# Holding an early store back until the last load has landed, in a log-sum-exp kernel that streams its input

One core of one Trainium2 chip. The metric is the device time of one execution in microseconds (us), median of several.

## The reference

The input is 32 x 512 rows of 1024 floats (67.1 MB), the output one float per row (65.5 KB).

```python
def reference(x):                       # x: (32, 512, 1024) float32
    max_x = np.max(x, axis=-1, keepdims=True)
    return (max_x.squeeze(-1) + np.log(np.sum(np.exp(x - max_x), axis=-1))).astype(np.float32)
```

## The kernel before

Each partition gets 128 rows ("columns" of the result): 112 from the first part of the input and 16 from the rest, so that the output is two contiguous blocks. SyncE issues 16 loads into a ring in SBUF, large ones first, of one row per partition at last. ScalarE takes the exponential without subtracting a maximum, VectorE or ScalarE sums, ScalarE takes Ln. A check at the end branches to a safe path if a sum is out of range (never taken here). What the change touches, cut:

```python
    for i, (size, ops) in enumerate(loads):
        ...
        dma = nc.sync.dma_start(out=ring[:, here : here + size], in_=source(done, size)).ins
        ...                                    # exponentials (line 143 with sum, 148 without), sums (160, 165)
        if c == LATE:                          # 119 columns are summed
            ln = nc.scalar.activation(out=res[:, 0:W], in_=sumexp[:, 0:W], func=AF.Ln)     # line 184, W = 112
            ...
    nc.at_finalize(wait_for_store_in_barrier)  # GpSimd, not SyncE, waits for last_store, in the closing barrier

    nc.scalar.activation(out=res[:, W:NC], in_=sumexp[:, W:NC], func=AF.Ln)               # line 232
    nc.sync.dma_start(out=out_rows, in_=res[:, 0:W])                                       # line 233, the first store
    last_store = nc.sync.dma_start(out=out_rest, in_=res[:, W:NC]).ins                     # line 234, the final store
```

SyncE executes its instructions in program order: 16 loads, first store, final store. In the loop's last turn `dma` is the last load.

## Time and profile before

| | before |
|---|---|
| time, median of the first 3 runs | 163.46 us (163.31 to 163.52) |
| span of the profiled execution | 161.5 us |
| queue q1 (all loads and stores), share of 16 engines | 97.1% |
| last load landed | 157.90 us |
| ScalarE busy without a gap from | 153.50 us |
| first store issued / landed | 150.80 / 158.1 us |
| final store issued / landed | 159.35 / 160.77 us |

Landing times in this table are the trace's own; the prediction below, which shows the lines and follows the end of the span back, adds figures rounded to 0.1 us and so has 157.87 and 160.75.

### The profile page before, as it was taken

What the parts mean: (1) busy time and instruction counts of PE and PEld (TensorE: products, weight loads), DVE (VectorE), ACT (ScalarE), POOL (GpSimd) and SP (SyncE); (2) the same over time, 40 slices, a digit from 0 to 9 for tenths busy, and PEclk for the clock granted to TensorE, in tenths of its full rate; (3) what the DMA queues carried; (4) which work ended last, traced back from release to release, by engine and by line L of the source; (5) the groups of instructions that cost most, each with busy time, mean ns of one, the idle gap of its engine ahead of it and who ended that gap; (6) DMA issues with size and microseconds to landing.
All of it is one profiled execution on the core that took longest, in us unless ns stands there. A gap on an engine that the chain in (4) does not pass through costs nothing.

```text
span 161.5 us, 257 instructions
## 1 busy us (share of the span) xinstructions
PE 1.9 (1%) x24; PEld 1.0 (1%) x24; DVE 114.9 (71%) x61; ACT 117.0 (72%) x59; POOL 0.2 (0%) x4
## 2 busy tenths in 40 slices
PE   0000000000000000000000000000000000000021
PEld 0000000000000000000000000000000000000011
DVE  0000000899929999399999999999499956996683
ACT  3000059990799609994299949974999999999994
POOL 0000000000000000000000000000000000000000
DMA  8997997997997997998899999997999999999990
GB/s 276 503 519 308 471 519 308 471 519 308 471 519 325 455 519 341 438 519 357 382 438 438 438 422 406 495 495 318 438 438 464 388 440 416 430 424 420 414 382 8
DMA packets 2594, 67.19 MB, mean 416 GB/s; under 512 B 544, under 2 KB 544, under 8 KB 928
## 3 DMA queue, kind: packets, MB, share of 16 engines
q1 hardware_dynamic: 2592, 67.18, 97.1%
q14 instruction: 2, 0.02, 0.0%
HBM read 67.11 MB, written 0.07 MB: 416 GB/s over the span
## 4 chain that ended last, share of the span: by engine, by line
DMA 59%; ACT 19%; DVE 16%; another core or an unknown queue 3%; issue 1%; SPq 0%; PE 0%
DMA ring<-in_x_dram 59%; ACT ring L148 19%; DVE sumexp L160 15%; DVE ring L165 1%; SPq L131 0%; DVE bad L238 0%; PE count L119 0%; DVE bad L239 0%; DVE fine L247 0%; PE count L246 0%; DVE clamped L115 0%; PE count L245 0%
## 5 line engine op out<-in xcount | busy, mean ns | idle before, releaser
L160 DVE TENSOR_REDUCE sumexp<-ring 128x8 f32<-128x8192 f32 (+6 forms) x17 | 102.9, 6107 | 39.6 <-ACT ring L148 39.6
L148 ACT ACTIVATE ring<-ring 128x8192 f32<-128x8192 f32 (+14 forms) x24 | 98.9, 4174 | 41.5 <-DMA ring<-in_x_dram 41.5
L143 ACT ACTIVATE ring<-ring 128x1024 f32<-128x1024 f32 x15 | 15.6, 1040 | 0.0
L165 DVE SCALAR_TENSOR_TENSOR ring<-ring 128x512 f32<-128x512 f32 x17 | 10.9, 687 | 3.5 <-ACT ring L148 3.5
L143 ACT ACTIVATION_READ_ACCUMULATOR ring<-ring 128x1 f32 x15 | 2.8, 186 | 0.0
L108 PE MATMUL count<-far,bad 128*1 128x1 f32 x2 | 0.2, 164 | 153.2 <-DVE clamped L104 153.2
L80 ACT ACT_TABLE_LOAD x1 | 1.3, 1283 | 0.8 <-PEq L309 0.8
L114 PE MATMUL count<-sumexp,ones 128*1 128x1 f32 x16 | 1.4, 164 | 3.9 <-DVE ring L165 3.9
L165 DVE DVE_READ_ACCUMULATOR ring<-ring 128x1 f32 x17 | 1.4, 82 | 0.0
L143 ACT ACTIVATE last_exp<-ring 128x1024 f32<-128x1024 f32 x1 | 1.0, 1005 | 0.0
L108 PEld LDWEIGHTS count<-far,bad 128*1 128x1 f32 x2 | 0.1, 80 | 153.2 <-DVE clamped L104 153.2
L114 PEld LDWEIGHTS count<-sumexp,ones 128*1 128x1 f32 x16 | 0.6, 81 | 4.6 <-DVE ring L165 4.6
L81 DVE MEMSET ones<- 128x1 f32 x1 | 0.1, 59 | 0.9 <-PEq L309 0.9
L247 DVE TENSOR_SCALAR fine<-count 1x1 int32<-1x1 f32 x1 | 0.1, 147 | 0.4 <-PE count L246 0.4
L104 DVE SCALAR_TENSOR_TENSOR clamped<-clamped,sumexp 128x119 f32<-128x119 f32 x1 | 0.3, 283 | 0.0
L238 DVE TENSOR_REDUCE bad<-ring 128x1 f32<-128x64 f32 x1 | 0.2, 220 | 0.1
L184 ACT ACTIVATE res<-sumexp 128x112 f32<-128x112 f32 x1 | 0.3, 278 | 0.0
L100 DVE TENSOR_SCALAR clamped<-sumexp 128x119 f32<-128x119 f32 x1 | 0.2, 221 | 0.0
L232 ACT ACTIVATE res<-sumexp 128x16 f32<-128x16 f32 x1 | 0.2, 215 | 0.0
L119 PE MATMUL count<-far,bad 128*1 128x1 f32 x2 | 0.2, 164 | 0.3 <-DVE clamped L115 0.3
L246 PE MATMUL count<-sumexp,ones 128*1 128x1 f32 x2 | 0.2, 164 | 0.0
L245 PE MATMUL count<-far,bad 128*1 128x1 f32 x2 | 0.2, 164 | 0.0
(13 smaller groups left out, 1.4 us busy)
## 6 DMA issues: line engine op xcount, KB each, us to landing
ring<-in_x_dram SPq DMA_DIRECT2D x1, 6912.0 KB, 31.7
ring<-in_x_dram SPq DMA_DIRECT2D x1, 6400.0 KB, 26.4
ring<-in_x_dram SPq DMA_DIRECT2D x1, 4608.0 KB, 25.1
ring<-in_x_dram SPq DMA_DIRECT2D x1, 3840.0 KB, 23.4
ring<-in_x_dram SPq DMA_DIRECT2D x1, 2816.0 KB, 25.8
ring<-in_x_dram SPq DMA_DIRECT2D x1, 2048.0 KB, 30.0
ring<-in_x_dram SPq DMA_DIRECT2D x1, 1792.0 KB, 22.5
ring<-in_x_dram SPq DMA_DIRECT2D x1, 1408.0 KB, 25.4
```

What stands on the lines that cost most here:

```text
L80: nc.scalar.preload_act_table_set("natural_log_exp_and_others")
L100: nc.vector.tensor_scalar(out=clamped[:, 0:LATE], in0=sumexp[:, 0:LATE], scalar1=LOW, scalar2=HIGH, op0=ALU.max, op1=ALU.min,)
L104: counted = nc.vector.scalar_tensor_tensor(out=clamped[:, 0:LATE], in0=clamped[:, 0:LATE], scalar=0.0, in1=sumexp[:, 0:LATE], op0=ALU.bypa ...
L108: nc.tensor.matmul(count, lhsT=bad[:, 0:1], rhs=far, start=True, stop=False)
L114: nc.tensor.matmul(count, lhsT=ones, rhs=sumexp[:, c : c + 1], start=False, stop=False)
L119: nc.tensor.matmul(count, lhsT=bad[:, 1:2], rhs=far, start=False, stop=False)
L143: exp = nc.scalar.activation(out=o, in_=v, func=AF.Exp, accum_out=sums)
L148: exp = nc.scalar.activation(out=v, in_=v, func=AF.Exp)
L160: added = [nc.vector.reduce_sum(out=sums, in_=rows, axis=AX.X)]
L165: nc.vector.scalar_tensor_tensor(out=lo, in0=lo, scalar=1.0, in1=rows[:, r, H:d], op0=ALU.mult, op1=ALU.add, accum_out=sums[:, r : r + 1],)
L184: ln = nc.scalar.activation(out=res[:, 0:W], in_=sumexp[:, 0:W], func=AF.Ln)
L232: nc.scalar.activation(out=res[:, W:NC], in_=sumexp[:, W:NC], func=AF.Ln)
```

## The change

Intent: "keeps its packets out of the last load's". The store of the first 112 columns, ready at 150.8 us while loads were still streaming, should not share the DMA engines with the last of them. It now waits for the last load, still ahead of the final store.

```diff
     nc.scalar.activation(out=res[:, W:NC], in_=sumexp[:, W:NC], func=AF.Ln)
-    nc.sync.dma_start(out=out_rows, in_=res[:, 0:W])
+    store = nc.sync.dma_start(out=out_rows, in_=res[:, 0:W]).ins
+    info = mybir.DependencyInfo(mybir.DependencyClass.Sync, mybir.DependencyReason.DATA)
+    tc.add_manual_dep(store, dma.name, info, reason="keeps its packets out of the last load's")
     last_store = nc.sync.dma_start(out=out_rest, in_=res[:, W:NC]).ins
```

## The prediction

> **What bounds the kernel now.** I read the page first, then the answers for the last 12 us, because the change touches only what SyncE does after it has issued all loads.
>
> The page says that the kernel is one stream of loads:
>
> ```profile
> GB/s 276 503 519 308 471 519 308 471 519 308 471 519 325 455 519 341 438 519 357 382 438 438 438 422 406 495 495 318 438 438 464 388 440 416 430 424 420 414 382 8
> q1 hardware_dynamic: 2592, 67.18, 97.1%
> HBM read 67.11 MB, written 0.07 MB: 416 GB/s over the span
> ```
>
> Loads and both stores are on one queue, q1, whose packets took 97.1% of 16 engines' span. Only the last of the 40 slices (4.04 us each) is empty: there the end is set by what follows the last data. The 0.07 MB written are both stores together, so all that the change can move is 0.056 MB out of 67.
>
> The DMA issues of the page give the two stores, and the source view of the load line over the last two issues gives the last two loads (their count and start, then time to landing, min/median/max):
>
> ```profile
> out_dram<-res SPq DMA_DIRECT2D x1, 56.0 KB, 7.3
> out_dram<-res SPq DMA_DIRECT2D x1, 8.0 KB, 1.4
> L131 SPq DMA_DIRECT2D ring<-in_x_dram x2: 327/380/432, 131.3 to 131.7; - x2
> DMA to landing us min/median/max: 25.4/25.8/26.2
> ```
>
> Asked for the issue at 131.30 alone, the DMA view gives 25.4, so the last but one landed at 131.30 + 25.4 = 156.70 and the last at 131.67 + 26.2 = 157.87. The gap, 1.17 us for 512 KB (0.524 MB), is 448 GB/s: the last load came at full rate, although the early store was outstanding.
>
> The timeline of ScalarE and of SyncE's queue from 153 us (start, duration, line):
>
> ```profile
> 153.50 3.50 ACT L148 ACTIVATE ring<-ring 128x2304 f32<-128x2304 f32 x2 [0.23 <-DMA ring<-in_x_dram]
> 156.91 1.04 ACT L143 ACTIVATE ring<-ring 128x1024 f32<-128x1024 f32 x1
> 157.85 0.19 ACT L143 ACTIVATION_READ_ACCUMULATOR ring<-ring 128x1 f32 x1
> 157.95 1.00 ACT L143 ACTIVATE last_exp<-ring 128x1024 f32<-128x1024 f32 x1
> 158.89 0.19 ACT L143 ACTIVATION_READ_ACCUMULATOR last_exp<-ring 128x1 f32 x1
> 159.11 0.21 ACT L232 ACTIVATE res<-sumexp 128x16 f32<-128x16 f32 x1
> ...
> 150.80 0.35 SPq L233 DMA_DIRECT2D out_dram<-res  x1
> 159.35 0.34 SPq L234 DMA_DIRECT2D out_dram<-res  x1
> ```
>
> From 153.50 on ScalarE runs back to back. Its last wait for a load is the 0.23 us before 153.50. The last row's exponential starts at 157.95, 1.04 us after the one before it, which is the plain spacing of this form on ScalarE (144.30, 145.33, 146.37 earlier in the timeline). Its data were there at 157.87. So the end runs: ScalarE busy from 153.50, Ln of the last 16 columns to 159.33, final store issued at 159.35, landed at 159.35 + 1.4 = 160.75, then the closing barrier to 161.5:
>
> ```profile
> L320 POOLq EVENT_SEMAPHORE  x4: 17/17/43, 160.8 to 161.4; - x4
> ```
>
> GpSimd's first barrier step, which holds the wait for the final store, begins at 160.8, just when that store has landed. The first store, issued at 150.80, landed at 150.80 + 7.3 = 158.1 and is on nobody's path.
>
> **What the Trainium skill says.** "DMA: Bandwidth & Descriptors", section Queues, rings and completion order: SP owns one queue row, and each DMA engine consumes that row's descriptors in ring order. So a store issued behind the last load should not start on an engine before that engine's share of the load. The trace agrees. The DMA view from 150.8 to 156.4:
>
> ```profile
> DMA packets 444, 2.29 MB, mean 410 GB/s; under 512 B 48, under 2 KB 48, under 8 KB 364
> ```
>
> Each DMA carries one packet of under 512 B per engine that counts its semaphore: on the whole page 544 = 18 DMAs x 16 + 128 rows of 448 B + 128 rows of 64 B. The 48 here are 3 loads x 16, so for 5.6 us after its issue not one packet of the store has moved.
>
> Same page, section Anatomy of one DMA: DMA engines do not wait on semaphores; the issuing sequencer does, before dispatch. So the new wait holds SyncE itself, and the final store behind it in SyncE's order. The trace of before agrees in kind: SyncE's own waits show it standing at the first store until ScalarE's Ln is done.
>
> ```profile
> SPq L233 <- ACT res L184: 12.6, 1, 12.6
> SPq L234 <- ACT res L232: 8.1, 1, 8.1
> ```
>
> Same page, same section: the fixed cost of a DMA is put at about 2 us (a fit for the GpSimd path), mostly the receipt of the write. Here a store from SyncE with nothing ahead of it took 1.4 us; I use that.
>
> **The change part by part.**
>
> Removed: nothing in work. The same 18 DMAs move the same bytes, and ScalarE, VectorE and TensorE get the same instructions.
>
> Added: a wait of SyncE for the last load at the first store, perhaps one semaphore instruction. It is passed at 157.87 instead of 150.80. Meanwhile SyncE has nothing else to do: the 8.1 us at the final store are pure standing.
>
> Moved, first store: issue from 150.80 to about 157.9, its issue instruction (0.35 us) done at 158.25. Landing: the 1.4 us of the final store, plus 48 KB more at 410 GB/s, 0.12 us, and for short rows perhaps twice that: 1.5 to 1.7 us, so 159.4 to 159.6 in place of 158.1.
>
> Moved, final store: it waits for ScalarE's 159.33. SyncE is free at 158.25, so the slack is 159.33 - 158.25 = 1.1 us. Not moved.
>
> Moved, closing barrier: SyncE must also see the first store landed. It needs that by about 160.7, where GpSimd comes in after the final store; 159.6 leaves 1.1 us. Not moved.
>
> Gained at the loads: the store's packets no longer lie beside the tail of the last load. The windows (width, each engine's busy us and count, clock, DMA share, GB/s) show where they lay:
>
> ```profile
> 156.80:157.00 0.20, 0.00 (x0) 0.00 (x0) 0.17 (x2) 0.20 (x2) 0.00 (x0) 1.00 0.85 323
> 157.00:157.20 0.20, 0.17 (x2) 0.09 (x2) 0.17 (x1) 0.20 (x1) 0.00 (x0) 1.00 0.86 301
> 157.20:157.40 0.20, 0.02 (x1) 0.00 (x0) 0.20 (x1) 0.20 (x1) 0.00 (x0) 1.00 0.49 144
> 157.40:157.60 0.20, 0.00 (x0) 0.00 (x0) 0.20 (x1) 0.20 (x1) 0.00 (x0) 1.00 0.19 49
> ```
>
> The engines finish over some 0.6 us; those that are done with their share of the load run the store, eight short rows each, while others still load. On any one engine the load comes first, so only a shared path could be relieved. The most that can be won is the whole store's bytes at the full rate, 0.057 MB / 410 GB/s = 0.14 us of an earlier landing (157.73 instead of 157.87). ScalarE would not use it, as it is busy until 157.95. Gain on the path: 0.
>
> Sum: 0 removed + 0 added on the path + 0 gained = 163.46 us, with the noise of the three runs, 163.31 to 163.52. I put it at 163.42, a hair under, for runs without the profiler in which the last load may come after ScalarE is free: there some of the 0.14 us could show.
>
> **The rivals.**
>
> The last load is really held up by the store, and ScalarE by the load. For it: data come at 157.87, only 0.08 us before ScalarE is free, so a run with slightly slower loads would be bound by them. Against it: 448 GB/s in the last gap and no idle time on ScalarE. It would make at most 0.14 us, so 163.3.
>
> The wait takes the place of what it removes: the first store delays the final one, through SyncE's order or because its packets and write receipts are still under way. For it: all is in one queue, and the two issues come from 8.5 to 1.45 us apart. Against it: the 1.1 us of slack, and the data of the final store move only at 160.2 to 160.4 (the window shows 40 GB/s there and none between 159.6 and 160.2), when the first store should have landed. A collision would cost 0.1 to 0.4 us: 163.55 to 163.9.
>
> The first store becomes the last thing to land. That needs a landing over 2.8 us after its issue (157.9 to 160.7), twice the measured 1.4. If it took 3.3 us, the end would move by 0.5 us: 164.0.
>
> A small one beside it: the trace shows 2 packets of instruction fetch, q14, at 159.0 to 159.6, where the queue was empty; now the first store's rows may lie near them, each a few hundredths of a us. They feed engines that reach the barrier before GpSimd does. No effect on the end.
>
> **Range and chances.** The mechanism gives 0 to -0.14 us on one side and, if a slack is misjudged, +0.1 to +0.5 us on the other; the runs scatter by 0.2 us. So 163.42 us, range 163.1 to 163.75. Two per cent is 3.3 us, over six times the worst rival, so faster 0.005, slower 0.01, same 0.985; what is left outside is a misread of the program's order.
>
> **What would show it right or wrong.** Right: the first store is issued at 157.9 and lands within 1.8 us; ScalarE has no idle time before the last exponential; the final store is still issued at about 159.35 and lands in 1.4 us; the span stays 161.5. The first step is wrong if the last load lands more than 0.14 us earlier relative to the one before it. The second is wrong if the final store is issued more than 0.05 us after ScalarE's last Ln, or takes clearly over 1.4 us. The prediction fails if a wait on ScalarE or VectorE is new, or if GpSimd's first barrier step no longer follows the final store's landing.

## The result

| | before | after |
|---|---|---|
| time, median of 6 | 163.37 us (163.17 to 163.52) | 163.54 us (163.52 to 163.72) |
| span of the profiled execution | 161.5 us | 161.7 us |
| first store issued / landed | 150.80 / 158.1 | 157.98 / 159.5 |
| final store issued / landed | 159.35 / 160.77 | 159.36 / 161.01 |

The ratio is 1.0013, 95% interval 1.0000 to 1.0025. (Ratios here are the mean time of one kernel's fast runs over that of the other's in the same rounds, so not quite the ratio of the medians.) Within 2% by far; if anything slower by 0.2 us.

Set side by side, the two programs have the same instructions in the same order on every engine; only the one wait is new. SyncE's queue after the change (start, duration, line):

```profile
157.98 0.35 SPq L233 DMA_DIRECT2D out_dram<-res  x1
159.36 0.34 SPq L236 DMA_DIRECT2D out_dram<-res  x1
```

SyncE's own waits after:

```profile
SPq L233 <- DMA ring<-in_x_dram: 25.8, 1, 25.8
...
SPq L236 <- ACT res L232: 0.9, 1, 0.9
```

The new wait stands where it was meant to, and 0.9 us of the final store's standing time are left: SyncE's order costs nothing. The last two loads, time to landing after the change (min/median/max):

```profile
DMA to landing us min/median/max: 25.3/25.8/26.2
```

The last load took 26.2 us from its issue, as before: **nothing was won at the load**, although the windows (width, busy us and count of each engine, clock, DMA share, GB/s) show that the store really left its tail and now moves at 158.8 to 159.2:

```profile
157.20:157.40 0.20, 0.02 (x1) 0.00 (x0) 0.20 (x1) 0.20 (x1) 0.00 (x0) 1.00 0.16 62
...
158.80:159.00 0.20, 0.01 (x1) 0.01 (x2) 0.13 (x3) 0.20 (x2) 0.00 (x0) 1.00 0.68 193
```

ScalarE's timeline after is that of before to within 0.01 us:

```profile
153.51 3.50 ACT L148 ACTIVATE ring<-ring 128x2304 f32<-128x2304 f32 x2 [0.24 <-DMA ring<-in_x_dram]
...
157.95 1.00 ACT L143 ACTIVATE last_exp<-ring 128x1024 f32<-128x1024 f32 x1
...
159.12 0.21 ACT L232 ACTIVATE res<-sumexp 128x16 f32<-128x16 f32 x1
```

What differs is the last step. The DMA issues after (KB, us to landing), and GpSimd's barrier steps:

```profile
out_dram<-res SPq DMA_DIRECT2D x1, 56.0 KB, 1.6
out_dram<-res SPq DMA_DIRECT2D x1, 8.0 KB, 1.7
```

```profile
L322 POOLq EVENT_SEMAPHORE  x4: 17/17/43, 161.0 to 161.6; - x4
```

The final store, issued at the same time, landed 1.7 us after its issue in place of 1.4, and the barrier began at 161.0 in place of 160.8. That is the whole of the span's 0.24 us. Its data moved at the same time as before (first packet at 160.19 in both traces). Of its 16 completions, one from each DMA engine, 15 came by 160.77 in both; the last at 160.77 before and at 161.01 after. **One DMA engine of 16 was late by a quarter of a microsecond.** The experiments ask whether that is real, and why.

### The profile page after: what moved, and what is told of

Read it like the earlier page. It is cut to its first block, busy times and chain, and to the rows that moved or that the text cites. A ratio compares the mean times of both kernels' runs of the same rounds, so it can differ in the third digit from the quotient of the medians.

```text
span 161.7 us, 257 instructions
## 1 busy us (share of the span) xinstructions
PE 1.9 (1%) x24; PEld 1.0 (1%) x24; DVE 114.9 (71%) x61; ACT 117.0 (72%) x59; POOL 0.2 (0%) x4
## 4 chain that ended last, share of the span: by engine, by line
DMA 59%; ACT 19%; DVE 16%; another core or an unknown queue 3%; issue 1%; SPq 0%; PE 0%
DMA ring<-in_x_dram 59%; ACT ring L148 19%; DVE sumexp L160 15%; DVE ring L165 1%; SPq L131 0%; DVE bad L240 0%; PE count L119 0%; DVE bad L241 0%; DVE fine L249 0%; PE count L248 0%; DVE clamped L115 0%; PE count L247 0%
```

## The experiments

Twelve runs, of the changed kernel again and of eleven others, all within the 2% that count as "same". Their times, each against the kernel before in the same rounds:

| run | us (lowest to highest) | before | ratio (95%) |
|---|---|---|---|
| after_again | 163.53 (163.41-163.63) | 163.31 | 1.0013 (1.0000-1.0027) |
| no_first | 163.28 (163.10-163.39) | 163.31 | 0.9999 (0.9985-1.0012) |
| early_and_late | 163.38 (163.28-163.50) | 163.31 | 1.0008 (0.9994-1.0022) |
| wait_last_but_one | 163.37 (163.08-163.44) | 163.31 | 1.0000 (0.9986-1.0014) |
| late_same | 163.64 (163.49-163.69) | 163.32 | 1.0018 (1.0004-1.0032) |
| late_high_half | 163.47 (163.35-163.58) | 163.32 | 1.0006 (0.9992-1.0019) |
| late_low_half | 163.36 (163.18-163.63) | 163.32 | 1.0007 (0.9993-1.0021) |
| late_later | 163.59 (163.46-163.90) | 163.32 | 1.0015 (1.0001-1.0029) |
| eight_behind | 163.93 (163.81-164.30) | 163.32 | 1.0042 (1.0026-1.0059) |
| from_gpsimd | 163.46 (163.33-163.83) | 163.32 | 1.0014 (0.9997-1.0031) |
| after_last_ln | 163.80 (163.77-163.83) | 163.32 | 1.0028 (1.0011-1.0045) |
| fetch_earlier | 163.65 (163.60-163.90) | 163.25 | 1.0023 (1.0011-1.0035) |

### Is it real: the changed kernel again

> The changed kernel again, because 163.54 against 163.37 us is hardly clear of the scatter. In its profile the final store landed 1.7 us after its issue at 159.36, before the change 1.4 us after 159.35, and nothing else on the path had moved. Theory A (a store that writes shortly before the final one makes the final one land late): ratio about 1.001, i.e. +0.15 to +0.25 us, and a landing of 1.6 to 1.7 us again. Theory B (chance in the landing of one store): ratio within 0.0005 of 1 and a landing anywhere from 1.4 to 1.7 us.

Ratio 1.0013 again, landing 1.7 us again, one completion late again (15 by 160.77, the last at 161.05). So theory B, chance, is unlikely: the two sets of runs, 11 in all, lie at 163.41 to 163.72, and their 15 runs of before at 163.15 to 163.52. The difference stays small beside the scatter: in the rounds of fetch_earlier the kernel before itself reached 163.60.

### The ceiling: no first store at all

```diff
-    nc.sync.dma_start(out=out_rows, in_=res[:, 0:W])
```

> The kernel before without its first store (112 of the 128 columns stay unwritten, so the result is wrong on purpose): the ceiling of what any placement of that store can win. The prediction's step says that its packets do not hold up the loads: last load landing 26.2 us after issue as before, ScalarE busy without a gap from 153.5 us, time within 0.1 us of the kernel before. The intent of the change (its packets are in the way of the last load) would have the last load land up to 0.14 us sooner. Theory A: final store lands in 1.4 us or less, since nothing was written before it.

Its output is wrong, which doesn't matter for the time. The time is that of before, and so are the last two loads (time to landing) and ScalarE:

```profile
DMA to landing us min/median/max: 25.3/25.8/26.2
```

```profile
157.89 1.00 ACT L143 ACTIVATE last_exp<-ring 128x1024 f32<-128x1024 f32 x1
```

The exponential before it starts at 156.85, so the spacing is 1.04 us and there is no gap. Without any first store the last load lands not 0.1 us sooner. **No placement of this store can win anything** that these runs could see (the interval reaches down to 0.9985, 0.25 us): that settles the intent of the change. The final store landed in 1.4 us here, although nothing was stored early.

### The wait without the move: wait for the last load but one

```diff
-    tc.add_manual_dep(store, dma.name, info, ...)
+    tc.add_manual_dep(store, last_but_one.name, info, ...)     # last_but_one: the dma of turn len(loads) - 2
```

> The changed kernel with the wait aimed at the last load but one, which landed at 156.70 us: the wait is there, but the packets of the store still come behind the last load's in the ring, at about 157.0 to 157.6 us as before the change. Theory A: landing of the final store 1.4 us, time as before the change (ratio within 0.0005 of 1). Theory C: +0.15 to +0.25 us, as in the change. Theory B: no difference.

The store was issued at 156.75 and its data moved at 157.6 to 157.9, a little later than expected; the final landing was 1.5 us and the median within 0.06 us of before. The interval just holds the change's 1.0013, so the time alone does not rule out theory C, that waiting costs in itself; but the final store was issued at 159.36 here and in the change, so the wait delays nothing that follows it on SyncE.

### The move without the wait's loss: an idle store at the late place

```diff
     nc.sync.dma_start(out=out_rows, in_=res[:, 0:W])
+    scratch = nc.dram_tensor("scratch", (P, W), fp32, kind="Internal").ap()
+    late = nc.sync.dma_start(out=scratch, in_=res[:, 0:W]).ins
+    tc.add_manual_dep(late, dma.name, info, ...)
```

> The kernel before, with a second store of the same 128 rows of 448 B, to a scratch tensor, at the place where the change puts the first one. The real first store stays early. Theory A: the final store lands in 1.6 to 1.7 us and the time rises by 0.15 to 0.25 us, as in the change; if only neighbouring addresses of the same output matter, it stays at 1.4 us. Theory C (the wait of SyncE itself costs, not the writes): +0.15 to +0.25 us too, but with the final store issued later than 159.36. Theory B: no difference.

Landing 1.5 us, ratio 1.0008 with an interval that holds both 1 and the change's 1.0013: not decided. The same with the real rows, sent twice to the same addresses (`out=out_rows` in place of `scratch`):

> The kernel before, with its first store sent a second time, same rows to the same addresses, at the place where the change puts it. The same to a scratch tensor gave a ratio of 1.0008 (0.9994 to 1.0022) and a final landing of 1.53 us, the change 1.0013 and 1.65 to 1.7. Theory A1 (the writes must be near the final store's, in the same output): landing 1.65 to 1.7 us, ratio 1.001 to 1.0015. Theory A2 (any write shortly before does it, and the scratch run was merely at the low end): landing 1.5 to 1.7, ratio about 1.001. Theory D (what the change costs is that the first store is missing early, not that it is there late): landing 1.4, ratio 1.000.

The time rose (1.0018, clear of 1), so a first store that is also there early does not help. That alone does not refute theory D, because this kernel sends one store more than the change; no_first does, where the early store is missing too and neither the landing nor the time rose. But the profile shows a landing of 1.5 us, not 1.65 to 1.7. In this profile the final store was also issued 0.08 us later, with all of the tail.

### Near in address? One half of the rows late

```diff
-    nc.sync.dma_start(out=out_rows, in_=res[:, 0:W])
+    nc.sync.dma_start(out=out_rows[0:64], in_=res[0:64, 0:W])
+    store = nc.sync.dma_start(out=out_rows[64:P], in_=res[64:P, 0:W]).ins      # late_low_half: the halves swapped
+    tc.add_manual_dep(store, dma.name, info, ...)
```

> First store in two halves: rows 0 to 63 early, rows 64 to 127 (whose addresses adjoin those of the final store) at the late place. Theory A1, nearness in address: landing of the final store 1.65 to 1.7 us, as in the change. Volume of late writes: half of the effect, 1.5 to 1.55 us. Chance: as before the change, 1.4 us.

> The mirror: rows 64 to 127 early, rows 0 to 63 (far from the final store's addresses) late. Theory A1: landing 1.4 us and ratio 1.000. Volume of late writes: 1.5 to 1.55 us, as the other half.

Landing 1.6 us with the adjoining half late, 1.4 with the far half; but the times, 1.0006 and 1.0007, do not tell the two apart, and the profiles are of the slowest run of the one (163.58) and the fastest of the other (163.18). Inconclusive.

### Nearer in time

```diff
     seen = nc.vector.reduce_max(...)
+    store = nc.sync.dma_start(out=out_rows, in_=res[:, 0:W]).ins
+    tc.add_manual_dep(store, seen.ins.name, info, ...)         # final store after it, as before
```

> The first store waits for VectorE's reduction at 158.65 us instead of for the last load: issued at about 158.7, its data move at about 159.5 to 159.9, only 0.3 us before those of the final store (160.2), in place of 1.05 us in the change. SyncE is free again at 159.05, so the final store's issue should stay at 159.35. Theory A with time as its measure: the final store lands later than in the change, 1.8 us or more, ratio above 1.0015. If nearness in time does not matter: 1.65 to 1.7 us and 1.0013. First store landing at about 160.3 us, still ahead of the final one.

The DMA issues of this run:

```profile
out_dram<-res SPq DMA_DIRECT2D x1, 56.0 KB, 2.3
out_dram<-res SPq DMA_DIRECT2D x1, 8.0 KB, 1.9
```

Both stores land late here, the first at 161.1; SyncE then stood 1.2 us for it in the barrier. Three of its timed runs lie at 163.46 to 163.59, two at 163.9, and the profile is of one of these two. It fits theory A; the next run doesn't.

### Right ahead of the final store

```diff
-    nc.scalar.activation(out=res[:, W:NC], ...)
+    last_ln = nc.scalar.activation(out=res[:, W:NC], ...)
+    tc.add_manual_dep(store, last_ln.ins.name, info, ...)      # the first store, in its old place in the program
```

> The first store waits for ScalarE's last Ln, still ahead of the final store: the slack of 1.1 us that the prediction gives SyncE is used up. Issue of the first at 159.36, of the final one at about 159.72 (+0.36 us, one issue), their data one right behind the other at 160.2 to 160.8. By the prediction's slack: time +0.36 us at least, so about 163.7; with theory A (late writes delay the final landing) 0.2 to 0.4 us more, 163.9 to 164.1. If the end were set by anything other than the final store's landing: less than +0.2 us.

SyncE's queue, and the DMA issues:

```profile
159.42 0.35 SPq L233 DMA_DIRECT2D out_dram<-res  x1
159.82 0.43 SPq L236 DMA_DIRECT2D out_dram<-res  x1
```

```profile
out_dram<-res SPq DMA_DIRECT2D x1, 8.0 KB, 1.5
```

The final issue comes 0.40 us after the first and takes 0.43 us in place of 0.34: together 0.49 us, and the time rose by 0.48 us (163.80 against 163.32). So the end does hang on the final store's issue, as the prediction said, and the slack that the change left is real. But here the first store's data end only 0.15 us before the final store's begin, in the change 1.03 us, and the landing is not late: 0.37 us after the last data packet, as before the change. All four runs lie within 0.06 us. **Theory A, that late writes as such delay the final landing, fails.**

### What does the lateness go with: instruction fetches

The DMA views show two packets of 8 KB on the instruction queue, q14, near the end. The second starts at about 159.4. Its length can be read from the view of 159.25 to 160.0 us, where it is the only packet of that queue: its share of 16 engines times 16 x 0.75 us. Before, after, and after again:

```profile
q14 instruction: 1, 0.01, 4.0%
```

```profile
q14 instruction: 1, 0.01, 6.1%
```

```profile
q14 instruction: 1, 0.01, 6.5%
```

That is 0.48 us before, 0.73 and 0.78 us in the two profiles of the changed kernel. With its start it ended at 159.91, 160.16 and 160.21; the final store's data begin at 160.19. All profiles, from the packets of the traces (us):

| run | late data to final data | second fetch to final data | last data packet to landing |
|---|---|---|---|
| before | 2.56 | 0.28 | 0.37 |
| no_first | none | 0.27 | 0.38 |
| wait_last_but_one | 2.28 | 0.21 | 0.46 |
| early_and_late | 1.06 | 0.22 | 0.49 |
| after, after_again | 1.03, 1.04 | 0.04, -0.02 | 0.60, 0.59 |
| late_same | 0.40 | 0.21 | 0.51 |
| late_high_half | 0.39 | 0.36 | 0.54 |
| late_low_half | 0.55 | 0.28 | 0.39 |
| late_later | -0.12 | 0.24 | 0.70 |
| eight_behind | 1.05 | 0.66 | 0.38 |
| after_last_ln | 0.15 | 0.77 | 0.37 |
| fetch_earlier | 1.06 | 0.67 | 0.41 |

(First column: from the end of the store ahead to the first packet of the final one. Second: from the end of the last fetch to it. For from_gpsimd, with its store long done, the last two are 0.54 and 0.37.) The first column does not order the third: 0.15 and 1.05 go with 0.37 and 0.38, 1.03 with 0.60. The second does better: from 0.27 up 0.37 to 0.41, at about 0.2 near 0.5, at zero 0.6. Two runs do not fit, late_high_half, and late_later, where the two stores overlap. The Trainium skill, "DMA: Bandwidth & Descriptors", section Queues, rings and completion order, gives a way: the increment that a DMA engine sends on completion lands only after every earlier write of that engine, across its queues. A fetch under way on one engine would then hold up exactly one completion of 16, which is what the traces show. The packets carry no engine number, so that it is the same engine has to be read from their times.

Their times show that a fetch holds up other packets. In late_same the store ahead has 128 rows, eight for each engine. The DMA views of 159.43 to 159.69 and of 159.69 to 159.88 us show nothing of it in the first stretch (the one packet is the second fetch) and nine packets in the other:

```profile
DMA packets 1, 0.01 MB, mean 32 GB/s; under 512 B 0, under 2 KB 0, under 8 KB 0
DMA packets 9, 0.00 MB, mean 19 GB/s; under 512 B 9, under 2 KB 9, under 8 KB 9
```

These nine are eight rows and a completion, one engine's whole share. They begin at 159.69, where the first fetch (159.19 to 159.70) ends; the other 15 engines were through at 159.43. In late_high_half and late_low_half four rows, one engine's share of half the store, begin in the same way at 159.68 and 159.42, as the first fetch ends (159.68, 159.42); in late_later five rows at 160.11, as the second ends (160.11). That may be why late_high_half and late_later do not fit: in them the store ahead itself landed late (160.72, 161.08), and the last completion of the final one came 0.17 to 0.18 us behind it.

The landing also keeps its distance from the second fetch. In eight profiles (before, no_first, wait_last_but_one, early_and_late, after, after_again, late_same, late_low_half) the final store landed 0.84 to 0.92 us after that fetch ended, whether it had ended 0.56 us after the final store's issue (before) or 0.86 us (after_again). In the other six it had ended 1.10 us or more before the landing.

The last run tried it:

```diff
     nc.vector.memset(far, 100 * HIGH)
+    idle = stats.tile([P, 1], fp32, name="idle")
+    for _ in range(2):
+        nc.scalar.activation(out=idle, in_=ones, func=AF.Exp)       # in the changed kernel
```

> The changed kernel with two idle exponentials of 128x1 at the start of ScalarE's program, to move an instruction fetch. In every profile so far the instruction queue moves one packet of 8 KB that starts between 159.3 and 159.8 us; its length goes with the final landing: 0.48 us long (4.0% of 16 engines in 159.25 to 160.0) and landing 1.4 us before the change, 0.73 and 0.78 us (6.1%, 6.5%), so ending at about 160.2 where the final store's data move, and landing 1.7 us in the two profiles of the changed kernel; only one engine of 16 is late there. An instruction more on VectorE (eight_behind) moved another such fetch from 159.1 to 156.7. Theory F (that fetch is in the way of the final store's last completion on one engine, and the moved store made it long): here the fetch comes at 156.5 to 158.5, nothing of the instruction queue is left after 159.3, the final store lands in 1.4 us and the ratio to the kernel before is 1.000 to 1.0005, unless the fetch now delays the last load. Theory A (late writes themselves): 1.65 to 1.7 us and 1.0013 again, although the fetch has moved. If the fetch does not move, the run says nothing.

Two instructions more at the start of ScalarE's program did move the fetch, farther than expected, to 151.57 us, amid the loads. The DMA issues, then ScalarE's timeline:

```profile
out_dram<-res SPq DMA_DIRECT2D x1, 56.0 KB, 1.6
out_dram<-res SPq DMA_DIRECT2D x1, 8.0 KB, 1.4
```

```profile
153.77 3.50 ACT L151 ACTIVATE ring<-ring 128x2304 f32<-128x2304 f32 x2 [0.61 <-DMA ring<-in_x_dram]
```

The final store lands in 1.4 us again although the first store is where the change puts it. Theory F's landing came true; theory A's 1.65 to 1.7 did not. The other fetch (159.1 before, here 159.35 with the later tail) stayed and ended at 159.79, 0.67 us ahead of the final data; the expectation that none is left was wrong. And the time did not come back: 0.32 us of one DMA engine at 151.6 are followed by a load that lands 0.27 us later than before (ScalarE waits until 153.77 in place of 153.50), so the loss only changed place. Counted from its issue that load landed after 28.2 us in place of 27.8, and in the trace one packet of the loads begins as the fetch ends, at 151.88, and takes 0.73 us where its neighbours take 0.35. One profile; it supports theory F and does not prove it.

### Does a store behind the last load hold it up, at any size?

```diff
     nc.sync.dma_start(out=out_rows, in_=res[:, 0:W])
+    scratch = nc.dram_tensor("scratch", (8, P, W), fp32, kind="Internal").ap()
+    nc.sync.dma_start(out=scratch.rearrange("k p w -> p k w"), in_=idle.rearrange("p (k w) -> p k w", w=W))
```

(`idle` is a zeroed tile, one instruction more on VectorE.)

> Does a store behind the last load hold it up? The kernel before, with one more store of 8 times as many rows of 448 B (459 KB, to a scratch tensor) right behind the first store, issued at about 151 us. If a store's packets start on each DMA engine only after the load ahead of them (the prediction's step): the last load lands 26.2 us after its issue as before, ScalarE has no gap after 153.5 us, and the small packets run on to about 159.3 us (8 x 8 packets of 25 ns per engine, 1.6 us more). If they mix with the loads: the last load lands up to 459 KB / 410 GB/s = 1.1 us later, ScalarE waits, time +1 us. The final store's own landing may rise by 0.1 to 0.3 us by the late writes.

The DMA view from 150.8 to 156.4 us, the last two loads, and ScalarE:

```profile
DMA packets 444, 2.29 MB, mean 409 GB/s; under 512 B 48, under 2 KB 48, under 8 KB 365
```

```profile
DMA to landing us min/median/max: 25.3/26.1/26.9
```

```profile
158.56 1.03 ACT L145 ACTIVATE last_exp<-ring 128x1024 f32<-128x1024 f32 x1 [0.60 <-DMA ring<-in_x_dram]
```

Half of each answer. The store's packets stay back as the ring order has it: 48 short packets, the same three loads' completions as before, and no row of a store. But the last load landed 26.9 us after its issue in place of 26.2, ScalarE waits 0.60 us, and the time rises by 0.6 us. By the packets' times this is one engine: the others were through with the load at 157.47. The extra instruction also moved a fetch to 156.72, and behind it, each packet beginning as the one before it ends, come the load's last three, which end at 157.42, 157.89 and 158.05. Two of them took 0.40 and 0.49 us, where 0.16 is usual. The fetch itself (0.31 us) explains a part of the delay. Whether the stores' rows, moving on the other engines from 157.00 on, slowed the two packets is not shown: the packet behind the fetch in fetch_earlier took twice its usual time too, with no store near, and here eight packets of the loads took 0.21 to 0.39 us at 155.9 to 156.6, before any row of a store moved. So the run does not show that a store holds up the load, and with 56 KB the effect is nil, as no_first shows.

### The store on another queue

```diff
-    nc.sync.dma_start(out=out_rows, in_=res[:, 0:W])
+    nc.gpsimd.dma_start(out=out_rows, in_=res[:, 0:W])
```

> The first store from GpSimd's queue instead of SyncE's, issued when Ln of the 112 columns is done (150.8 us): its packets are on another ring and can mix with the loads at once. If only the order within one ring keeps the store away from the loads: small packets of that queue appear at about 152 us and the loads after it land about 0.1 to 0.2 us later (56 KB at 410 GB/s is 0.14 us); ScalarE has 0.08 us of slack at the last load and none at the one of 153.5, so time +0.05 to +0.2 us. If a small store costs the loads nothing: ratio 1.000.

The store's packets now lie amid the loads: 16 of 3,584 B at 154.9 to 155.8 us, their completions by 155.9. ScalarE:

```profile
156.86 1.04 ACT L143 ACTIVATE ring<-ring 128x1024 f32<-128x1024 f32 x1
...
157.99 1.03 ACT L143 ACTIVATE last_exp<-ring 128x1024 f32<-128x1024 f32 x1
```

Spacing 1.13 us in place of 1.04, so ScalarE stood 0.09 us for the last load, which landed 26.3 us after its issue. The slack of 0.05 us (157.90 to 157.95) is used up and a little shows. The time, 1.0014 with an interval that holds 1, can't confirm so small an effect. That the order of one ring protects the loads from a small store rests on this one profile.

## Why the prediction was right or wrong

It was right in what it was asked: 163.54 us lies in 163.1 to 163.75, and the class is "same". By its steps:

- **Nothing is won at the loads: right.** 26.2 us with the store behind the last load, after it, or absent. ScalarE without a gap in all three.
- **First store, landing in 1.5 to 1.7 us: right.** 1.6 us from 157.98.
- **Final store and SyncE's order, "Not moved": right for the issue** (159.36, with 0.9 us of standing left), and using the slack up costs what the step says (after_last_ln, +0.48 us).
- **Closing barrier, "Not moved": wrong in size.** SyncE saw the first store in time, as the step says, but the step, like the one before it, took the final store's 1.4 us as fixed. It was 1.7 us in both profiles of the changed kernel, which is the prediction's own sign that this part is wrong ("takes clearly over 1.4 us"). That term, +0.24 us in the span, is why the time is 0.2 us above the kernel before and not 0.04 us below. The second rival, a collision of 0.1 to 0.4 us that ends at 163.55 to 163.9, had the size. Its cause, the first store's writes still under way, failed as a general one: with the writes right ahead of the final store the landing was not late. The range allowed for a misjudged slack, and no slack was misjudged, so that it held the result is partly luck.
- **The instruction fetch, "No effect on the end": probably the step that failed.** The prediction asked only whether the engines that are fed are on the path, not which DMA engine the fetch occupies, and it put the two fetches at 159.0 to 159.6, where their packets last to 159.91. The lateness goes with a fetch that ends when the final store's data move, and went when a fetch was moved away.
- **Two readings are rounded:** in the trace's own figures the last two loads land at 156.66 and 157.90, so the gap is 1.24 us or 423 GB/s, not 448, and ScalarE's slack is 0.05 us, not 0.08. Still full rate (the mean is 416), still no wait.

Open: why the fetch took 0.73 to 0.78 us in the changed kernel and 0.31 to 0.55 us in the others at that place, and so whether the moved store made it long or its length is chance in two profiles; and whether fetch and late completion share a DMA engine, which only the times suggest. In late_high_half and late_later a second cause, the nearness of the writes, isn't ruled out.

None of the versions beats the kernel before.

## What to carry to other kernels

The store behind the last load in the same ring did not take its place in line (26.2 us to landing with and without it). So before moving a transfer, delete it and look whether the load lands sooner: if not, no placement helps. A store that ends the kernel is finished when the slowest of its DMA engines is: here one of 16, late by 0.24 us, moved the end by 0.24 us, and an instruction fetch is the likely reason. An added instruction can move such fetches (to 156.7 and 151.6 us here), and at the scale of 0.3 us this can outweigh the change that one is studying.

## What the Trainium skill lacked or had wrong

- "Runtime: NRT & Kernel Launch", section Instruction fetch mechanics: it calls the cost of a fetch mostly hidden, and names blocks of 16 KiB. Here the late fetches are packets of 8 KB that moved separately, 0.31 to 0.78 us each on one DMA engine (by the packets' times); after one at 151.6 us a load landed 0.27 us later. No page says that a fetch can delay a load or a store's completion.
- "DMA: Bandwidth & Descriptors", section Queues, rings and completion order: the order within a ring keeps a store from starting before the load ahead of it on the same engine, as the page says (for 5.6 us after its issue no row of the store moved). It does not say what a fetch costs the packets of other queues on its engine: one engine's rows waited until the fetch ended (159.42 to 160.11 us in four profiles), and the packet behind it took 0.40 us in place of 0.16 or 0.73 in place of 0.35 in two others.
- "DMA: Bandwidth & Descriptors", section Anatomy of one DMA: the fixed cost of about 2 us is a fit for the GpSimd path, and the section has no such figure for SyncE. From SyncE, with the queue idle, an 8 KB store landed in 1.4 us and a 56 KB one in 1.6 us.
